# Retention queries of a hybrid decoder trunk: projected two token tiles at a time with channels on the partitions, and one sine table kept in SBUF

## The chip, the core and the metric

The kernel runs on one core of a Trainium2 chip. TensorE (PE) multiplies, VectorE (DVE), ScalarE (ACT) and GpSimd (POOL) work elementwise, SyncE (SP) issues most of the DMAs; each engine runs its own queue of instructions in order and waits on semaphores for the others. SBUF has 128 partitions; matmul results land in PSUM. The metric is the device time of one execution in microseconds (us); of several runs the median is given. The large products use the 32-bit type f32r, and to keep float32 accuracy each operand is split into a high and a low part and multiplied in three passes.

## What is computed

A trunk of two layers on 1024 tokens of 1024 channels. Each layer normalises x, projects it once into all the heads' inputs, runs three groups of heads (sliding-window attention, retention, gated linear attention) and projects their outputs back. The change touches retention: four heads of 64 channels, rotated by position, with a decay of its own per head.

```python
def apply_rotary(x, positions, inv_freq):
    ang = positions[..., None] * inv_freq
    cos, sin = jnp.cos(ang), jnp.sin(ang)
    x1, x2 = jnp.split(x, 2, axis=-1)
    return jnp.concatenate([x1 * cos - x2 * sin, x2 * cos + x1 * sin], axis=-1)

def step(state, inp):
    qi, ki, vi = inp
    sc = jnp.einsum('bhid,bhjd->bhij', qi, ki) * dmask
    intra = jnp.einsum('bhij,bhjv->bhiv', sc, vi)
    inter = jnp.einsum('bhid,bhdv->bhiv', qi * q_decay, state)
    new_state = chunk_decay * state + jnp.einsum('bhjd,bhjv->bhdv', ki * k_decay, vi)
    return new_state, intra + inter
...
rq = apply_rotary(rq.reshape(B, S, RET_HEADS, RET_DK), positions, ret_freq)
rk = apply_rotary(rk.reshape(B, S, RET_HEADS, RET_DK), positions, ret_freq)
r = retention(rq, rk, rv.reshape(B, S, RET_HEADS, RET_DV))
r_out = rms_norm(r).reshape(B, S, RET_W) * jax.nn.silu(rg)
```

`step` runs over chunks of 128 tokens. The attention's queries and keys are rotated in the same way with other frequencies.

## The kernel before

The tokens are 8 tiles of 128, in 4 pairs. For each pair the normalised tokens lie transposed in SBUF (channels on partitions, `hT`), as a high and a low part. A projection of one tile to 256 columns (`project`) keeps the token tile stationary and moves the weights: 3 passes over 8 blocks of channels, 24 matmuls of 256 columns, with tokens on the partitions of the result. `project_T` does the opposite for attention and gated linear attention: weights stationary, tokens moving, channels on the partitions of the result.

A layer runs through stages: the gates (`do_gates`: the columns rg and gg, silu by tanh), retention, gated linear attention, attention, output. In the retention stage (the loop at the end of the printed part of `layer`) each pair takes rq, rk and rv for its two tiles. `ret_rot` (L1154) rotates q and k with the tokens on partitions (`rotary`, five VectorE operations L823 to L828) and multiplies by the decay of the token within its chunk (L1157, tables qdec and kdec). `ret_core` (L1160) is a job for each tile: it transposes q and k on TensorE (two 128-wide transposes each, helper L180), copies all four out of PSUM in one 512-wide copy on ScalarE (helper L149, "rT"), makes the scores (helper L165, out of which VectorE takes the causal part, L1179), then the output po from the state stR and from the scores times v, and brings the state up to date (L1198, L1200). The output is normalised by head in `head_norm_gate`, with `rstd_of` (L632) for the reciprocal root.

The sines and cosines of all positions (`tables`, L411) are made once, while layer 0's gates run: one multiplication, 13 steps that reduce the angle, two sines on ScalarE (L438, L439, with a load of the function table), and two operations for the cosine. They lie in `sincos` with tokens on partitions; columns 0 to 31 of each tile are attention's, 32 to 63 retention's. For attention's queries, which lie with channels on partitions, `tables_T` (L444) copies each pair's sines four times over (L449), transposes them on TensorE (4 times 4), and stores them in DRAM (`tabS`); `attn_rot` loads them from there for every half (L864).

The order of TensorE's instructions is written by hand. The program counts a clock `clk` of TensorE's own work; jobs (Python generators) yield how long after the present clock they may go on, from the table `L`, and flags say what must have been reached. `pump()` lets those jobs run that are due, every `CHUNK` = 7 matmuls of a projection and after each projection. The order of the other engines' queues is set by the Tile framework's scheduler from priorities and its own estimates, so that an edit in one place moves instructions elsewhere. Buffers come from tagged pools: `t2` (512 wide), `t1` (256 wide), `aux` and `mm` (PSUM banks), `arena` (weights and tokens as high and low parts). Weights come by DMA into `st` and are split there: the high part by a copy on ScalarE (L149) or VectorE (L151), the low part by a subtraction (L533). The tokens of tiles 4 to 7 are normalised (`pre`) while the gates of the tiles before them run: squares L651, transposes L180, scale and shift L698 (ScalarE, first half) and L700 (VectorE, second half), high part L704, low part L708.

## Time and profile before

| | before |
|---|---|
| runs | 996.72, 998.21, 999.19 us; median 998.21 |
| profiled execution | 996.31 us, span of the trace 994.6 us, granted TensorE clock 0.991 |
| TensorE, VectorE, ScalarE, GpSimd busy | 965.7, 683.2, 409.3, 246.3 us |
| TensorE matmul records | 7133, of which 128-wide transposes (L180) 292 |
| gate stage of layer 0 | about 50 to 100 us |
| retention stage | about 103 to 195 us (layer 0), 595 to 676 us (layer 1) |

How to read the rows in the next parts: a window row gives the stretch, its length, then the busy time and instruction count of PE, PEld (weight loads, which overlap), DVE, ACT and POOL, then the granted clock, the share of the DMA engines, and GB/s. A timeline row gives the start, the duration, the engine, the source line, the operation, out<-in and how many instructions stand together; in brackets is how long the engine was idle just before and what it waited for. A row of the waits names the engine and line that waited, what for, the us in all, how often, and the longest. A row of the groups ends in the busy time, the mean duration in ns, and the idle time before.

### The profile page before, as it was taken

To read this page: it belongs to the slowest core of one execution; us is meant where nothing else is said; L and a number is where in the kernel's file an instruction comes from. 1 tells how busy PE (TensorE), PEld (TensorE's weight loads), DVE (VectorE), ACT (ScalarE), POOL (GpSimd) and SP (SyncE) were. 2 spreads that over 40 slices of the span, in tenths; PEclk is the share of its full clock that TensorE was granted. 3 is DMA by queue.
4 is the path that set the end of the run, shared out by engine and by line. 5 is a ranking of instruction groups with operands and counts; after the bars stand their busy time and mean duration, and the time that the engine had idled before them with its cause. 6 is when DMAs were issued, how large, how long until landed. Compare 5 with 4: busy or idle time off the path is not lost.

```text
span 994.6 us, 19641 instructions
## 1 busy us (share of the span) xinstructions
PE 965.7 (97%) x7133; PEld 824.3 (83%) x7133; DVE 683.2 (69%) x1679; ACT 409.3 (41%) x1152; POOL 246.3 (25%) x310
## 2 busy tenths in 40 slices
PE   5899999999999999999999999999999999999996
PEld 1599999888998777778889999988999877777785
DVE  3779857677766777664677286775766577567876
ACT  2477312233332656632555332133333257574222
POOL 2322001233310234420124101113322034545000
PEclk8899999999999999999999999999999999999999
DMA  9843513523135355587555241352122434378883
GB/s 321 290 138 97 159 44 115 177 86 121 61 100 166 91 157 168 170 274 239 189 170 171 69 150 38 118 157 83 53 93 86 127 91 133 112 235 266 267 262 139
DMA packets 112305, 148.77 MB, mean 150 GB/s; under 512 B 12065, under 2 KB 63821, under 8 KB 112209
## 3 DMA queue, kind: packets, MB, share of 16 engines
q1 hardware_dynamic: 106512, 137.96, 44.5%
q10 hardware_dynamic: 5696, 9.56, 2.6%
q8 instruction: 56, 0.92, 0.4%
q14 instruction: 41, 0.33, 0.1%
HBM read 109.20 MB, written 36.18 MB: 146 GB/s over the span
## 4 chain that ended last, share of the span: by engine, by line
PE 80%; DVE 7%; DMA 7%; issue 2%; POOL 1%; ACT 1%; SPq 0%; ACTq 0%; POOLq 0%; DVEq 0%
PE mm L165 61%; PE aux L165 14%; PE aux L180 5%; DMA st<-in_w_in_dram 2%; POOL sm L635 1%; DMA t<-aoS 1%; DMA st<-in_w_last_dram 1%; DMA xk<-in_x_dram 1%; DVE arena L533 1%; DMA a<-mixS 1%; DVE t L1248 0%; DVE t L328 0%; DMA t<-in_x_dram 0%; DMA t<-xs 0%; DMA mixS<-t 0%
## 5 line engine op out<-in xcount | busy, mean ns | idle before, releaser
L165 PE MATMUL mm<-arena 128*128 128x256 f32 (+2 forms) x1824 | 299.9, 318 | 1.8 <-ACT arena L704 1.8
L165 PE MATMUL mm<-arena,arena 128*128 128x256 f32 (+2 forms) x1824 | 298.2, 316 | 0.0
L165 PEld LDWEIGHTS mm<-arena 128*128 128x128 f32 x1824 | 255.5, 191 | 26.0 <-issue 3.3
L165 PEld LDWEIGHTS mm<-arena,arena 128*128 128x128 f32 x1824 | 252.2, 188 | 24.3 <-issue 3.7
L635 POOL TENSOR_TENSOR sm<-sm,mhalf 128x1 f32<-128x1 f32 (+1 forms) x64 | 55.8, 872 | 335.9 <-DVE sm L634 317.8
L165 PE MATMUL mm<-arena,mx 128*128 128x512 f32 (+1 forms) x564 | 130.6, 387 | 0.5 <-ACT kept L1341 0.5
L165 PEld LDWEIGHTS mm<-arena,mx 128*128 128x128 f32 x564 | 101.4, 188 | 24.7 <-issue 1.9
L149 ACT ACTIVATE t<-aux 128x256 f32<-128x256 f32 (+2 forms) x124 | 55.8, 468 | 73.8 <-PE aux L180 62.2
L149 ACT ACTIVATE arena<-st 128x512 fp32r<-128x512 f32 x94 | 56.2, 627 | 53.2 <-DMA st<-in_w_in_dram 19.4
L929 POOL TENSOR_TENSOR smx<-smx,sm 128x512 f32<-128x512 f32 x32 | 36.1, 1129 | 125.7 <-DVE sm L928 118.0
L533 POOL TENSOR_TENSOR arena<-st,arena 128x512 fp32r<-128x512 f32 x31 | 42.7, 1378 | 79.7 <-ACT arena L149 72.9
L533 DVE TENSOR_TENSOR arena<-st,arena 128x512 fp32r<-128x512 f32 x77 | 58.0, 775 | 5.2 <-ACT arena L149 3.3
L925 ACT ACTIVATE smx<-smx,sm 128x129 f32<-128x129 f32 x128 | 49.9, 393 | 25.9 <-DVE sm L922 25.7
L364 DVE SCALAR_TENSOR_TENSOR acc<-st,c_act,acc 128x512 f32<-128x512 f32 x60 | 46.7, 778 | 16.9 <-DMA st<-in_w_mod_dram 16.5
L180 PE MATMUL aux<-c_ident,t 128*128 128x128 f32 (+1 forms) x292 | 48.2, 282 | 5.4 <-DVE t L666 5.0
L180 PEld LDWEIGHTS aux<-c_ident,t 128*128 128x128 f32 (+1 forms) x292 | 35.0, 144 | 12.4 <-DVE t L666 6.9
L698 ACT ACTIVATE t<-aux,mod,mod 128x128 f32<-128x128 f32 x68 | 25.9, 459 | 43.0 <-DVE t L1248 18.1
L165 PEld LDWEIGHTS aux<-t,mx 32*128 32x128 f32 (+1 forms) x896 | 39.5, 187 | 3.9 <-issue 2.1
L973 ACT ACTIVATE t<-aux 128x256 f32<-128x256 f32 x32 | 12.3, 383 | 73.6 <-PE aux L165 65.0
L165 PE MATMUL aux<-t,mx 32*128 32x32 f32 (+1 forms) x896 | 40.7, 272 | 0.0
L920 DVE COPY_PREDICATED smx<-c_curmask,aux 128x256 f32<-128x256 int32 x64 | 25.4, 446 | 19.5 <-ACT smx L149 17.2
L1248 DVE SCALAR_TENSOR_TENSOR t<-t,sm,t 128x512 f32<-128x512 f32 x32 | 24.0, 780 | 18.2 <-DMA t<-in_x_dram 10.8
(224 smaller groups left out, 1387.7 us busy)
## 6 DMA issues: line engine op xcount, KB each, us to landing
st<-in_w_in_dram SPq DMA_DIRECT2D x96, 256.0 KB, 3.8
st<-in_w_mod_dram SPq DMA_DIRECT2D x64, 256.0 KB, 3.1
mx<-mixS SPq DMA_DIRECT2D x20, 512.0 KB, 4.9
mixS<-t SPq DMA_DIRECT2D x72, 128.0 KB, 3.7
st<-in_w_last_dram SPq DMA_DIRECT2D x36, 256.0 KB, 3.8
wm<-in_w_mod_dram SPq DMA_DIRECT2D x12, 512.0 KB, 7.0
t<-in_x_dram SPq DMA_DIRECT2D x24, 256.0 KB, 4.9
t<-tabS SPq DMA_DIRECT2D x16, 256.0 KB, 4.6
```

The costliest lines, as they stand in the source:

```text
L149: A.activation(dst, src, AF.Copy)
L165: T.matmul(dst, lhsT, rhs, start=start, stop=stop)
L180: T.transpose(dst, src, idn)
L364: V.scalar_tensor_tensor(acc, wt, c_act[:, k:k + 1], acc, ALU.mult, ALU.add)
L533: e.tensor_tensor(lo, st, f(hi), ALU.subtract)
L635: G.tensor_tensor(r, r, mhalf[:, :w], ALU.pow)
L698: A.activation(hf[:, ks], at[kt], AF.Identity, scale=gain, bias=shift)
L920: V.copy_predicated(sv, curmask.unsqueeze(1).to_broadcast((P, 2, P)), pv[:, :, n // P - 1, :])
L925: A.activation(sm[:, h, :], sm[:, h, :], AF.Exp, bias=mx[:, h:h + 1], accum_out=sums[:, h:h + 1])
L929: eng("pn").tensor_tensor(sm[:, :, 0:128], sm[:, :, 0:128], rs.unsqueeze(2).to_broadcast((P, 4, P)), ALU.mult)
L973: A.activation(sq, po, AF.Square)
L1248: V.scalar_tensor_tensor(xt[j], yg[j], r, xt[j], ALU.mult, ALU.add)
```

## The change

- Retention's queries are projected for a pair at once, with weights stationary and the pair's 256 tokens moving (`project_P`), so that the result has channels on partitions: two halves of 128 channels, 24 matmuls of 256 columns each. q is no longer transposed.
- The rotation of that result (`ret_q`) exchanges the two 32-channel halves of each head, that is, blocks of 32 partitions. Four VectorE products of 32 partitions by 512 read one block of PSUM and write the neighbouring block of SBUF; one 512-wide product with the cosines and one addition complete it. The result goes into a tile that borrows the buffer of attention's keys (tag kT0 or kT1).
- The decays leave q and k. A token's output only scales with q's decay and is normalised by head afterwards, so that the decay goes into the eps of that norm (`reps`); k's decay is put on v (`vdec`), where the ScalarE copy of v becomes a VectorE product.
- The copy of the transposed keys is 256 wide in place of 512 for q and k, and it and the causal product have high priority.
- `sincos` is transposed as it is (8 transposes in place of 16, no copies), stored to `tabS`, read back into `tab` (SBUF, 1 MB, four DMAs) for retention, and copied from DRAM to DRAM into `tabA` (two DMAs) for attention.
- The tables are made earlier (tb1 6.0 in place of 24.5) in one buffer of another pool.

```diff
     def tables():
-        ang = t2()
-        V.tensor_tensor(ang.rearrange("p (t k) -> p t k", t=NT), posf.unsqueeze(2).to_broadcast((P, NT, 64)),
-                        freq.unsqueeze(1).to_broadcast((P, NT, 64)), ALU.mult)
+        tmp = mix_tile(F32).rearrange("p a k q -> p (a k q)").rearrange("p (i n) -> p i n", i=4)
+        ang, nn, n2, red = (tmp[:, i] for i in range(4))
+        with tc.issue_after(mark[3].ins):
+            V.tensor_tensor(ang.rearrange("p (t k) -> p t k", t=NT), posf.unsqueeze(2).to_broadcast((P, NT, 64)),
+                            freq.unsqueeze(1).to_broadcast((P, NT, 64)), ALU.mult)
...
     def tables_T():
-        for p in range(NP_):
-            yield L["tt1"]
-            rep_ = t2()
-            V.tensor_copy(rep_.rearrange("p (s t h k) -> p s t h k", s=2, t=2, h=4),
...
+        for i in range(2):
+            yield L["tt1"] if i == 0 else L["tt2"]
             pt = aux()
-            for i in range(4):
-                transp(pt[:, i * P:(i + 1) * P], rep_[:, i * P:(i + 1) * P], ident)
+            for t in range(4):
+                transp(pt[:, t * P:(t + 1) * P], sincos[:, 4 * i + t].rearrange("p s k -> p (s k)"), ident)
             tb = t2()
             A.activation(tb, pt, AF.Copy, scale=0.125)
-            nc.sync.dma_start(tabS[p], tb.rearrange("p (s n) -> p s n", s=2))
+            ts = slice(512 * i, 512 * i + 512)
+            nc.sync.dma_start(tabS[:, :, :, ts].rearrange("s c k n -> (s c k) n"), tb)
+        yield L["tt3"]
+        for b in range(4):
+            nc.sync.dma_start(tab[32 * b:32 * b + 32], tabS[:, 1].rearrange("s k n -> k s n"))
+        yield 20.0
+        for j in range(2):
+            nc.sync.dma_start(tabA[:, :, j], tabS[j, 0].unsqueeze(0).to_broadcast((4, 32, S)))
...
+    def project_P(pm, l, p, w, c):
+        h = hT[(l, p)]
+        accum(pm, lambda a, k: w[:, a, k, c:c + P], lambda b, k: h[:, b, k, 0:256])
+
     def rstd_of(ss, w, scale, eps):
         r = small(w)
-        V.tensor_scalar(r, ss, scale, eps, ALU.mult, ALU.add)
+        if isinstance(eps, float):
+            V.tensor_scalar(r, ss, scale, eps, ALU.mult, ALU.add)
+        else:
+            V.scalar_tensor_tensor(r, ss, scale, eps, ALU.mult, ALU.add)
...
-            nc.sync.dma_start(d.rearrange("p (s n) -> p s n", s=2),
-                              tabS[2 * hf:2 * hf + 2, :, s, :].rearrange("s p n -> p s n"))
+            nc.sync.dma_start(d, tabA[:, :, s, 512 * hf:512 * hf + 512].rearrange("h k n -> (h k) n"))
...
-    def ret_rot(t, src, dec_):
+    def ret_q(l, p, w):
+        pm = mm()
+        for c in range(2):
+            project_P(pm[:, 256 * c:256 * c + 256], l, p, w, c * P)
+
+        def two(x):
+            return x.rearrange("p (c n) -> p c n", c=2)
+
+        sn, cs = (tab[:, i, 256 * p:256 * p + 256].unsqueeze(1).to_broadcast((P, 2, 256)) for i in range(2))
+        u, x = t2(), t2()
+        for b in range(4):
+            r = slice(32 * b, 32 * b + 32)
+            o = two(x)[32 * (b ^ 1):32 * (b ^ 1) + 32]
+            if b % 2:
+                V.scalar_tensor_tensor(o, two(pm)[r], -1.0, sn[r], ALU.mult, ALU.mult)
+            else:
+                V.tensor_tensor(o, two(pm)[r], sn[r], ALU.mult)
+        V.tensor_tensor(two(u), two(pm), cs, ALU.mult)
+        if p % 2 == 0:
+            rqT[0] = gp.tile([P, NT * P], F32, tag=f"kT{p // 2}", name=nm("rq"), bufs=1)
+        q = rqT[0][:, 512 * (p % 2):512 * (p % 2) + 512]
+        V.tensor_tensor(q, u, x, ALU.add)
+        flag(("rq", l, p), L["rq1"])
+        return two(q)
...
+    def ret_k(t, src):
         r = t1()
         rotary(r, src, 4, t, 1)
-        eng("rdec").tensor_tensor(h4(r), h4(r), dec_.unsqueeze(2).to_broadcast((P, 4, 64)), ALU.mult)
         return r

     def ret_core(l, t, q, k, v):
         yield lat("rc1", l)
         pt = aux()
         for j in range(2):
-            transp(pt[:, j * P:(j + 1) * P], q[:, j * P:(j + 1) * P], ident)
-            transp(pt[:, (2 + j) * P:(3 + j) * P], k[:, j * P:(j + 1) * P], ident)
-        tt_ = t2()
-        qT = tt_[:, 0:256]
-        kTt = tt_[:, 256:512]
-        copy("rT", tt_, pt)
+            transp(pt[:, j * P:(j + 1) * P], k[:, j * P:(j + 1) * P], ident)
+        kTt = t1()
+        with tc.high_priority():
+            copy("rT", kTt, pt[:, 0:256])
+        yield (0.0, ("rq", l, t // 2))
+        qT = q[:, :, P * (t % 2):P * (t % 2) + P]
...
                     if name == "rv":
                         v = t1()
-                        copy("rv", v, src)
+                        V.tensor_tensor(h4(v), h4(src), vdec.unsqueeze(2).to_broadcast((P, 4, 64)), ALU.mult)
...
-L = {... "tt1": 8.0, "tt2": 1.75, "tb1": 24.5, ...}
+L = {... "tt1": 7.0, "tt2": 2.0, "tt3": 2.0, "tb1": 6.0, "rq1": 6.5, ...}
```

The retention loop calls `ret_q` once per pair, ahead of the four projections of rk and rv. Lines behind the change have higher numbers (L698 becomes L708, L704 L714, L990 L999, L1198 L1234).

Three places where instructions move are shown. The first is ScalarE's queue in layer 0's gate stage, around the normalised tokens of tiles 4 and 5 (their high parts go into arena_320 before, arena_322 now). Before:

```order
L990 ACTIVATE t_138_770<-mm_700 128x256
L698 ACTIVATE t_143_797<-aux_792,mod_10_120,mod_11_121 128x128 x4
L651 ACTIVATE t_146_816,sm_818<-t_73_373 128x512
L704 ACTIVATE arena_320<-t_143_797 128x4x128
L651 ACTIVATE t_147_817,sm_818<-t_74_374 128x512
L704 ACTIVATE arena_320<-t_145_809 128x4x128
L990 ACTIVATE t_152_842<-mm_775 128x256
L1008 ACTIVATE gaT_417<-aux_867 48x128
```
And now, with the load of the sines' table, the two sines into `sincos`, and the load back for the tanh:

```order
L439 ACT_TABLE_LOAD
L439 ACTIVATE sincos<-mx_512 128x8x64
L440 ACTIVATE sincos<-mx_512 128x8x64
L708 ACTIVATE t_143_816<-aux_811,mod_10_122,mod_11_123 128x128 x2
L999 ACT_TABLE_LOAD
L999 ACTIVATE t_151_859<-mm_796 128x256
L714 ACTIVATE arena_322<-t_143_816 128x4x128
L661 ACTIVATE t_146_835,sm_837<-t_73_375 128x512
L661 ACTIVATE t_147_836,sm_837<-t_74_376 128x512
L1017 ACTIVATE gaT_419<-aux_881 48x128
L708 ACTIVATE t_156_896<-aux_891,mod_10_122,mod_11_123 128x128 x2
L714 ACTIVATE arena_322<-t_145_828 128x4x128
```
The table work now stands ahead of tile 5's two high parts; before, it stood some twenty rows behind them. On TensorE the gate projections of tiles 4 and 5 (mm_864 and mm_936) have the two groups of table transposes in between:

```order
L165 MATMUL mm_864<-arena_71,arena_322 128x272 x7
L180 MATMUL aux_891<-c_ident,t_132_748 128x128 x4
L180 MATMUL aux_903<-c_ident,t_133_749 128x128 x4
L165 MATMUL mm_864<-arena_71,arena_322 128x272 x3
L180 MATMUL aux_918<-c_ident,sincos 128x128 x4
L165 MATMUL mm_936<-arena_71,arena_322 128x272 x7
L180 MATMUL aux_944<-c_ident,ga_708 48x128
L165 MATMUL mm_936<-arena_71,arena_322 128x272 x14
L180 MATMUL aux_961<-c_ident,t_146_835 128x128 x4
L180 MATMUL aux_973<-c_ident,t_147_836 128x128 x4
L180 MATMUL aux_985<-c_ident,sincos 128x128 x4
L165 MATMUL mm_936<-arena_71,arena_322 128x272 x3
```
Before, tile 5's projection was broken there only by one transpose of the low-rank columns (ga), and the table's sixteen transposes came later.

The second place is VectorE in layer 0's retention, the query block of pair 3 (mm_2049 is the projection, rq_1851 the result) and the update of the state stR behind tile 4:

```order
L151 CAST arena_322<-st_2177 128x512
L536 TENSOR_TENSOR arena_322<-st_2177,arena_322 128x512
L1179 TENSOR_TENSOR t_354_2137<-mm_2049,tab 32x512
L1177 SCALAR_TENSOR_TENSOR t_354_2137<-mm_2049,tab 32x512
L1179 TENSOR_TENSOR t_354_2137<-mm_2049,tab 32x512
L1177 SCALAR_TENSOR_TENSOR t_354_2137<-mm_2049,tab 32x512
L1180 TENSOR_TENSOR t_353_2136<-mm_2049,tab 128x512
L1234 TENSOR_TENSOR stR<-stR,aux_2159 64x2x64
L1184 TENSOR_TENSOR rq_1851<-t_353_2136,t_354_2137 128x512
L1234 TENSOR_TENSOR stR<-stR,aux_2159 64x2x64
L984 TENSOR_REDUCE sm_2169<-t_359_2167 128x4
L1236 TENSOR_TENSOR stR<-stR,c_cdt 128x256
```
The update of stR (L1234, L1236) has the weights' cast and subtraction and five operations of the query block ahead of it in the queue.

The third is ScalarE at the end of layer 1's retention: the weights' high parts (arena_71, arena_320) and the copies of the transposed q and k of tiles 6 and 7 (t_1462, t_1475). Before:

```order
L149 ACTIVATE arena_71<-st_8316 128x2x256
L149 ACTIVATE t_1455_8232<-aux_8229 128x256
L149 ACTIVATE t_1456_8235<-aux_8229 128x256
L149 ACTIVATE t_1459_8248<-mm_8203 128x256
L149 ACTIVATE t_1462_8263<-aux_8258 128x512
L149 ACTIVATE t_1469_8302<-mm_8250 128x256
L149 ACTIVATE arena_320<-st_8363 128x512
L149 ACTIVATE t_1475_8323<-aux_8318 128x512
L149 ACTIVATE arena_320<-st_8380 128x512
L149 ACTIVATE arena_320<-st_8392 128x512
```
Now, with the key copies t_1431 and t_1444:

```order
L149 ACTIVATE arena_71<-st_8134 128x2x256
L149 ACTIVATE t_1424_8101<-aux_8098 128x256
L149 ACTIVATE t_1425_8104<-aux_8098 128x256
L149 ACTIVATE t_1431_8130<-aux_8127 128x256
L149 ACTIVATE arena_71<-st_8152 128x2x256
L149 ACTIVATE arena_71<-st_8183 128x2x256
L149 ACTIVATE t_1444_8188<-aux_8185 128x256
L982 ACTIVATE t_1448_8209<-aux_8194 128x256
L149 ACTIVATE arena_322<-st_8241 128x512
```
The key copy of tile 6 now stands ahead of two of the conversions into arena_71, and that of tile 7 ahead of the first into the other arena, behind which t_1475 stood before.

More of the change, by code (lines that the diff above doesn't have):

```diff
@@ L262, in trunk @@
     srS = dr.tile([NT, P, 256], F32, name="srS")
-    tabS = dr.tile([NP_, P, 2, 256], F32, name="tabS")
+    tabS = dr.tile([2, 2, 32, S], F32, name="tabS")
+    tabA = dr.tile([4, 32, 2, S], F32, name="tabA")
+    tab = cp.tile([P, 2, S], F32, name="tab")
     modc = {}
@@ L1203, in ret_core @@
         dma("lsr", sg, srS[t])
-        yield from head_norm_gate(l, t, po[:, 0:256], sg, 4.0 / 64.0, 4.0 * EPS, 4)
+        yield from head_norm_gate(l, t, po[:, 0:256], sg, 4.0 / 64.0, reps, 4)
     def y_half(l, t, nh, mixt, ss, yg):
@@ L1503, in layer @@
             last = p == NP_ - 1
-            rr = {}
-            for name in ("rq", "rk", "rv"):
+            q = ret_q(l, p, used(l, "rq"))
+            pump()
+            if last:
+                load(l, "gqk")
+            ks = {}
+            for name in ("rk", "rv"):
                 w = used(l, name)
```

36 lines of the change are left out of this document (16 added, 20 removed).

## The prediction

> **What bounds the kernel now.** I read the page first (span, busy shares, the chain's shares), then TensorE's waits, then the windows of the stages that the change touches, then the timelines at the places where a wait stands or may come.
>
> ```profile
> span 994.6 us, 19641 instructions
> PE 965.7 (97%) x7133; PEld 824.3 (83%) x7133; DVE 683.2 (69%) x1679; ACT 409.3 (41%) x1152; POOL 246.3 (25%) x310
> PE 80%; DVE 7%; DMA 7%; issue 2%; POOL 1%; ACT 1%; SPq 0%; ACTq 0%; POOLq 0%; DVEq 0%
> ```
>
> TensorE is busy for 97% of the span and 80% of the chain that ended last. So a matmul taken off shortens the time by itself, and work on any other engine costs something only where TensorE must wait for it. The windows say where that is near.
>
> ```profile
> core 0: us, PE busy (x) PEld busy (x) DVE busy (x) ACT busy (x) POOL busy (x), PEclk, DMA share, GB/s
> 65.00:70.00 5.00, 5.00 (x45) 5.00 (x44) 3.99 (x12) 5.00 (x15) 1.48 (x2) 1.00 0.74 225
> 70.00:75.00 5.00, 5.00 (x43) 4.98 (x42) 4.67 (x15) 4.76 (x15) 0.63 (x2) 1.00 0.13 43
> 100.00:170.00 70.00, 70.00 (x599) 67.84 (x598) 49.92 (x155) 16.45 (x34) 7.00 (x6) 1.00 0.34 105
> 170.00:200.00 30.00, 28.71 (x218) 26.50 (x217) 21.54 (x60) 9.57 (x20) 7.93 (x6) 1.00 0.53 161
> 595.00:660.00 65.00, 65.00 (x556) 63.18 (x556) 46.24 (x145) 14.97 (x31) 8.32 (x8) 1.00 0.26 81
> 660.00:680.00 20.00, 17.58 (x113) 14.79 (x113) 10.91 (x25) 6.10 (x15) 4.59 (x4) 1.00 0.56 167
> ```
>
> Retention runs from about 103 to 195 us and from 595 to 676 us. In its body TensorE never stops (70.00 of 70.00, 65.00 of 65.00), VectorE has 29% to spare and ScalarE 77%. Idle stands only at its two ends: 1.3 us after 170, 2.4 us after 660. The gate stage at 65 to 75 us is another case: TensorE is full there too, but ScalarE has 0.24 us of 10 free and VectorE 1.3 us. Whatever is added there runs into the end of the stretch.
>
> **The matmuls.** The unit prices are two pieces of the chain.
>
> ```profile
> 103.60 4.83 PE mm L165 x41
> 108.42 0.44 PE aux L180 x4
> ```
>
> A 256-wide product takes 4.83/41 = 0.118 us, a 128-wide transpose 0.11. The query projection has 24 products of 256 columns per tile before; now it has 24 for each of two channel halves over the pair's 256 tokens: 48 for a pair either way, cost nothing. The transposes of q go: 2 per tile, 8 tiles, 2 layers = 32. The tables take 8 transposes in place of 16. 40 x 0.11 = **-4.4 us**, and with TensorE full I see no cover that could swallow it other than a new wait.
>
> **The waits at the end of retention.**
>
> ```profile
> PE aux L165 <- ACT t L149: 3.0, 3, 1.3
> 192.83 0.71 PE L165 MATMUL aux<-t 64*128 64x128 f32 x8 [1.29 <-ACT t L149]
> 663.09 0.71 PE L165 MATMUL aux<-t 64*128 64x128 f32 x8 [0.54 <-ACT t L149]
> 669.66 0.71 PE L165 MATMUL aux<-t 64*128 64x128 f32 x8 [1.22 <-ACT t L149]
> 191.39 0.63 ACT L149 ACTIVATE arena<-st 128x512 fp32r<-128x512 f32 x1 [1.14 <-DMA st<-in_w_in_dram]
> 668.49 0.63 ACT L149 ACTIVATE arena<-st 128x512 fp32r<-128x512 f32 x1 [3.71 <-DMA st<-in_w_in_dram]
> 669.03 0.58 ACT L149 ACTIVATE t<-aux 128x512 f32<-128x512 f32 x1
> ```
>
> All three are scores that wait for the copy of the transposed q and k. At 669.03 it is seen why: the copy stands on ScalarE behind a weight conversion that waited 3.71 us for its DMA; at 191.39 the same with 1.14 us. Those copies were ready long before. In the changed order the key copy (256 wide) of the last tiles stands ahead of those conversions, in both layers. So the sum of the three, 1.29 + 0.54 + 1.22, goes: **-3.0 us**, with 0 as the other bound if the copy's own inputs (the transposes, which TensorE's hand-made order now places elsewhere) come no earlier, or if the scores then wait for the query block. I take all of it since the cause seen at 668.49 is an order and the order is changed.
>
> **VectorE in retention.**
>
> ```profile
> L823 DVE TENSOR_TENSOR t<-mm,sincos 128x256 f32<-128x256 f32 (+1 forms) x48 | 17.7, 369 | 6.0 <-ACT va L851 4.0 <-PE mm L165 1.9
> L825 DVE TENSOR_TENSOR tr<-mm,sincos 128x128 f32<-128x128 f32 (+1 forms) x48 | 12.3, 256 | 0.0
> L827 DVE TENSOR_TENSOR t<-t,tr 128x128 f32<-128x128 f32 (+1 forms) x48 | 12.6, 263 | 0.0
> L1157 DVE TENSOR_TENSOR t<-t,c_qdec 128x256 f32<-128x256 f32 x16 | 6.7, 418 | 0.2
> L870 DVE TENSOR_TENSOR t<-mm,t 128x512 f32<-128x512 f32 x16 | 11.0, 688 | 15.5 <-PE mm L165 11.8 <-DMA t<-tabS 3.6
> L873 DVE TENSOR_TENSOR t<-t,t 128x512 f32<-128x512 f32 x8 | 8.5, 1057 | 0.0
> L1198 DVE TENSOR_TENSOR stR<-stR,aux 64x128 f32<-64x128 f32 x28 | 7.9, 281 | 0.2
> 67.98 1.29 DVE L708 TENSOR_TENSOR arena<-t,arena 128x512 fp32r<-128x512 f32 x2 [1.01 <-ACT arena L704]
> 73.08 0.69 DVE L708 TENSOR_TENSOR arena<-t,arena 128x512 fp32r<-128x512 f32 x1
> ```
>
> One tile's rotation of q or k is 0.369 + 2 x 0.256 + 2 x 0.263 = 1.41 us (L826 and L828 repeat L825 and L827), with the decay 1.83. A pair has four: 7.3. Now a pair has two rotations of k without decay (2.8), two multiplications of v from PSUM, 256 wide (2 x 0.42 by L1157), and six 512-wide operations for q: 6 x 0.69 by L870 = 4.1. Together 7.8, so **+0.5 us per pair**; a pair lasts 17.5 us, of which 5 are free on VectorE, and ScalarE loses work. Hidden, cost nothing in the sum.
>
> What no row shows is a product of 32 partitions that is written to another block of partitions. Below: L1198 on 64 partitions takes 0.281 for 128 elements against L825's 0.256 on 128 partitions, so fewer partitions buy nothing, 0.69 stands as the floor. Above: L873, the slowest 512-wide row on this engine, 1.06. I take 0.69, since L870 has the same operands (PSUM and SBUF).
>
> The block does stand in a queue. In pairs 2 and 3 of layer 0 its first five operations come ahead of the update of the state stR, on which the next tile's output product waits. Back to back a 512-wide operation takes 1.29 - 0.69 = 0.60. VectorE needs 5 x 0.60 + 2 x 0.28 + 0.60 + 0.42 = 4.6 us from the end of the projection to the new state; TensorE's order gives it about 4.1 (24 products of the next projection, an output, a state product, a 512-wide row sum): short by 0.5. In pair 3 TensorE gives some 0.8 more, but a cast and a subtraction for the weights (about 1.0) stand in front of it: short by 0.7 to 1.1. The bounds are 0 (what stands ahead is done before the projection ends) and 1.7; I take **+0.8**. In layer 1 the updates stand ahead of the block: nothing.
>
> [...]
>
> **The sine table, moved.** This is the term that I trust least.
>
> ```profile
> 55.96 1.86 SPq L154 DMA_DIRECT2D srS<-t  x2
> 63.41 0.63 ACT L149 ACTIVATE arena<-st 128x512 fp32r<-128x512 f32 x1 [3.10 <-DMA st<-in_w_in_dram]
> 71.37 0.64 ACT L704 ACTIVATE arena<-t 128x512 fp32r<-128x512 f32 x1
> 72.87 0.64 ACT L704 ACTIVATE arena<-t 128x512 fp32r<-128x512 f32 x1 [0.24 <-DVE t L700]
> 73.68 1.49 PE L165 MATMUL mm<-arena,arena 128*128 128x272 f32 x10
> 76.31 0.68 DVE L423 SCALAR_TENSOR_TENSOR t<-t,t 128x512 f32<-128x512 f32 x1
> 72.75 0.42 DVE L418 TENSOR_SCALAR t<-t 128x512 f32<-128x512 f32 x1
> 86.47 1.28 ACT L1023 ACT_TABLE_LOAD   x1
> 87.76 0.63 ACT L1023 ACTIVATE t<-t 128x512 f32<-128x512 f32 x1
> 89.71 0.63 ACT L438 ACTIVATE sincos<-t 128x512 f32<-128x512 f32 x1
> 90.24 0.62 ACT L439 ACTIVATE sincos<-t 128x512 f32<-128x512 f32 x1
> ```
>
> Before, the 14 operations that reduce the angles lie between 69 and 88 us, and the two sines at 89.71, with slack behind them. Now they stand at some 53 to 72 us in VectorE's order, 9 of L423's kind and 5 of L418's: about 9 x 0.60 + 5 x 0.34 = 7.1 us pushed into the queue that also makes the low halves of the normalised tiles. On ScalarE a table load, the two sines and a load back (1.28 + 1.15 + 1.28 = 3.7 us) now stand between the second half of tile 4 and the first half of tile 5. In the window 65 to 75 that engine had 0.24 us free. TensorE needs tile 5's high half three products into the row at 73.68, at 74.0; before it was there at 71.37 + 0.64 = 72.0. The second half, there at 72.87 + 0.64 = 73.5, is used four products later, at 74.5. So the margins are 2.0 and 1.0 us, and 3.7 us of ScalarE plus the delay of VectorE are laid on them.
>
> A walk through both queues with these durations: the second query chunk may land earlier than 63.41, since its issue now stands ahead of the two stores that took 1.86 us; I take half of that, 62.5. ScalarE then reaches tile 4's second half at about 70.5 (it waits for VectorE's scaling, now behind the table), ends the sines at 72.9 and tile 5's halves at 75.8 and 78.8. TensorE comes to tile 5 at 74.9 (after 0.6 of wait for tile 4's low half and 0.4 for the four 128-wide transposes of the table), waits 0.9 for the first half, 2.5 for the second, and 0.6 for a PSUM bank at the second set of transposes. With the transposes counted above, the waits are 0.6 + 0.9 + 2.5 + 0.6 = **+4.6 us**. Bounds: 0, if ScalarE's queue is in fact ahead when the chunk does not hold it; 8.5, if the chunk lands at 63.4 (+0.9) and VectorE's operations with two SBUF inputs stretch as L873 does against L870 (9 x 0.37 = +3.3).
>
> [...]
>
> The rest costs nothing: the eps tables are constants in the same number of operations, the one SBUF table takes 1 MB of DMA and the attention's tables another 1 MB where the share is 0.13 to 0.34, and attention loads as many bytes as it did.
>
> **Sum.** -4.4 - 3.0 + 0.8 + 4.6 = -2.0 us. The profiled execution took 996.31 (span 994.6), so 994.3; the median of the runs, 998.21, lies 1.9 above it: **996.2 us**.
>
> **Rivals.** *The early waits do not come.* The walk rests on one chunk's landing and on the order in which two full queues get through; if the chunk lands 2 us earlier, or part of the table work falls into VectorE's gaps ahead of 63, that term shrinks to nothing: -6.6, **991.6**. For it: TensorE was 100% busy in every one of these windows. Against it: ScalarE's 0.24 free us.
>
> *The waits at the end of retention stay*, because the scores wait for what else is late there (the decayed v, the query block, the mask product): the -3.0 falls away, +1.0, **999.2**.
>
> *The early stage costs its upper bound.* Landing at 63.4 and stretched table operations, waits of 8.5: -4.4 - 3.0 + 0.8 + 8.5 = +1.9, **1000.1**; it ends slower than before once the waits there pass 6.6.
>
> *The crossing products cost the price of L873.* Slower than before, at one place: 4 x (1.06 - 0.60) = 1.8 us more in each block, which in pairs 2 and 3 of layer 0 stands directly ahead of stR: waits of 0.6 + 1.8 and 1.1 + 1.8 in place of the 0.8 taken, +4.5, so +2.5 in all, **1000.7**. It decides from 0.74 us per product back to back, if the two waits come whole (1.7 + 2 x 4 x 0.14 = 2.8, which with -4.4, -3.0 and 4.6 is nothing). For it: nothing here crosses partitions, and L873 shows 512-wide operations that are slow; against it: L873's operands are both in SBUF, these are not.
>
> **How the numbers follow.** Forecast 0.36 (its own range 994 to 998.5); early waits absent 0.29; end waits stay 0.12; early stage at its bound 0.12; crossing products 0.11. From 990.5 (the second case with the last waits of 0.3 to 0.4 us gone too) to 1002 (the slower cases with a microsecond more each) some 0.2 is left outside. 0.3%, 3.0 us, is what a measurement of this kernel tells from no change: faster is below 995.2, slower above 1001.2. Faster: the second case and 0.16 of the forecast, 0.45. Slower: half of the two cases at 1000 and 0.06 from the others' tails, 0.16. Same: 0.39.
>
> **What would show it.** 1: L180 on TensorE falls from 292 to 252. 2: no wait for L149's copy near 190, 663 and 669. 3: waits of 0.5 to 2.5 us for ScalarE's high halves between 70 and 80 us, a table load and two sines just before, about 4.6 in all; if that window is full, the second case. 4: the products of 32 partitions at 0.6 to 0.7 us; at 1.0 or more, the slower case. 5: a wait for stR in layer 0 under 1.2. Wrong altogether if TensorE idles at a new place in the body of retention, where I have put nothing.

## The result, and the profile after

The changed kernel takes 1011.73 us (median of 6 runs, 1009.15 to 1015.91) against 997.81 (996.56 to 999.19): a ratio of 1.0141, with a 95% interval of 1.0121 to 1.0160. It is slower by 14 us; forecast were 996.2 us and a range of 990.5 to 1002. The profiled execution took 1009.24 us, 12.9 more than the one before.

The page of the changed kernel, the lines on the span and the engines:

```profile
span 1007.5 us, 19483 instructions
PE 967.5 (96%) x7093; PEld 823.9 (82%) x7093; DVE 694.0 (69%) x1627; ACT 399.3 (40%) x1135; POOL 249.2 (25%) x310
```

The 40 matmul records less (7133 to 7093) are the transposes that were to go. Yet TensorE is busy 1.8 us longer, and idle for 40.0 us of the span in place of 28.9. What it waited for stands in the view of TensorE's waits (us in all, times, longest):

```profile
PE aux L180 <- DVE t L676: 6.6, 4, 4.0
PE mm L165 <- ACT arena L149: 6.3, 1, 6.3
PE mm L165 <- ACT arena L714: 4.6, 3, 1.8
PE aux L165 <- DVE stR L1236: 1.2, 2, 0.8
PE aux L165 <- ACT t L149: 1.1, 1, 1.1
PE mm L165 <- DVE t L1001: 1.0, 2, 0.7
PE mm L165 <- DVE t L1180: 0.9, 2, 0.6
PE aux L180 <- DVE mx L1130: 0.7, 1, 0.7
PE aux L165 <- DVE sm L281: 0.6, 1, 0.6
PE aux L180 <- DVE sincos L443: 0.4, 1, 0.4
PE mm L165 <- DVE arena L718: 0.3, 1, 0.3
```

The second row is new and the longest of all outside the start: one wait of 6.3 us for a weight that ScalarE splits. 1.8 us of the third row stood at 40 us before as well. The windows answer to those of the prediction:

```profile
65.00:70.00 5.00, 4.35 (x37) 4.13 (x37) 5.00 (x10) 4.59 (x15) 2.67 (x4) 1.00 0.46 140
70.00:75.00 5.00, 3.77 (x28) 3.32 (x28) 4.64 (x13) 3.98 (x7) 0.59 (x2) 1.00 0.23 77
100.00:170.00 70.00, 63.39 (x514) 61.13 (x513) 45.06 (x108) 11.31 (x25) 5.37 (x5) 0.93 0.31 100
170.00:200.00 30.00, 29.52 (x253) 28.74 (x251) 23.48 (x61) 6.25 (x14) 5.90 (x5) 1.00 0.37 115
595.00:660.00 65.00, 64.35 (x549) 62.10 (x548) 46.37 (x116) 11.03 (x26) 4.68 (x5) 1.00 0.28 84
660.00:680.00 20.00, 19.99 (x165) 19.25 (x165) 17.28 (x43) 5.04 (x11) 3.42 (x3) 1.00 0.39 120
```

The gate stage at 65 to 75 us has lost 1.9 us, as forecast. But the body of layer 0's retention, 100 to 170 us, which was full, has lost 6.6 us, and its mean granted clock is 0.93. This is the sign that the prediction named for being wrong altogether: TensorE idles at a new place in the body of retention.

TensorE's timeline shows where:

```profile
72.48 1.26 PE L165 MATMUL mm<-arena,arena 128*128 128x272 f32 x8 [0.94 <-ACT arena L714]
...
77.86 0.77 PE L165 MATMUL mm<-arena,arena 128*128 128x272 f32 x4
80.45 0.64 PE L165 MATMUL mm<-arena,arena 128*128 128x272 f32 x3 [1.83 <-ACT arena L714]
...
114.37 0.94 PE L165 MATMUL mm<-arena,arena 128*128 128x256 f32 x6 [0.28 <-DVE t L1180]
121.57 5.66 PE L165 MATMUL mm<-arena,arena 128*128 128x256 f32 x25 [6.26 <-ACT arena L149]
```

The first row is a wait for tile 4's second high half, ready at 71.80 + 0.63 = 72.43 in ScalarE's rows below; the walk had none there. The third is the wait for tile 5's second high half (79.77 + 0.63 = 80.40), 1.83 for the forecast 2.5. For tile 5's first half, ready at 77.80, TensorE did not wait: it came to it only at 77.86, behind the first set of table transposes. The last row is in the second rk projection of the first pair. ScalarE and SyncE's queue show the weight chunk for which it waited:

```profile
71.80 0.63 ACT L714 ACTIVATE arena<-t 128x512 fp32r<-128x512 f32 x1
72.45 1.28 ACT L439 ACT_TABLE_LOAD   x1
73.74 0.63 ACT L439 ACTIVATE sincos<-mx 128x512 f32<-128x512 f32 x1
75.61 1.28 ACT L999 ACT_TABLE_LOAD   x1
77.18 0.62 ACT L714 ACTIVATE arena<-t 128x512 fp32r<-128x512 f32 x1
79.77 0.63 ACT L714 ACTIVATE arena<-t 128x512 fp32r<-128x512 f32 x1
...
120.88 0.63 ACT L149 ACTIVATE arena<-st 128x512 fp32r<-128x512 f32 x1 [9.75 <-DMA st<-in_w_in_dram]
```

```profile
105.82 1.39 SPq L461 DMA_DIRECT2D tabA<-tabS  x2
107.25 0.63 SPq L154 DMA_DIRECT2D st<-in_w_in_dram  x1
```

The last quarter of the weights of rk was issued at 107.25 and used by ScalarE at 120.88: 13.6 us, where such loads before took 3.8 in the median from issue to landing:

```profile
st<-in_w_in_dram SPq DMA_DIRECT2D x96, 256.0 KB, 3.8
```

It stands directly behind the two copies into `tabA`. The view of the DMA engines over 112 to 119 us, in 40 slices (tenths of the 16 engines' time, and GB/s):

```profile
DMA  9756996774433222222223222222222576889743
GB/s 375 281 152 176 269 281 257 269 246 176 176 129 129 117 94 117 117 94 94 94 94 140 94 117 117 94 94 94 117 117 94 152 176 199 246 316 339 304 176 152
```

For half of that time two to three tenths of the engines are busy, at about 100 GB/s, while the weight chunk is awaited. The view gives only the mean of the engines; a share of a quarter would be 4 of 16, and `tabA`'s copies have 4 repeats as their outermost dimension. At 100 GB/s the 1 MB takes 10 us: about the delay of the chunk. That these copies lie on 4 engines is my estimate from the share and the 4 repeats; no view lists the engines one by one. Where loads of weights stand nearly alone, 123.5 to 126.5 us, the same view has slices of nine tenths and more.

The wait has a second price, in windows of 2 us (the clock stands before the last two numbers):

```profile
114.00:116.00 2.00, 1.03 (x7) 0.77 (x6) 2.00 (x8) 0.00 (x0) 0.00 (x0) 1.00 0.27 109
116.00:118.00 2.00, 0.00 (x0) 0.00 (x0) 1.68 (x6) 0.00 (x0) 0.00 (x0) 0.70 0.38 123
118.00:120.00 2.00, 0.00 (x0) 0.00 (x0) 0.00 (x0) 0.00 (x0) 0.00 (x0) 0.50 0.47 182
122.00:124.00 2.00, 2.00 (x11) 2.00 (x11) 1.95 (x2) 0.00 (x0) 1.44 (x1) 0.50 0.12 45
```

The granted clock falls to 0.50 in the wait and is still there when TensorE works again: 11 products in 2 us, and the 25 products at 121.57 take 5.66 us in place of 25 x 0.118 = 2.95. That is 2.7 us more. The last product before the wait ended at 114.37 + 0.94 = 115.31, and the clock fell about 1.5 us later (1.00 over 115 to 116 us, 0.90 on average over 116 to 117, 0.50 from 117 on).

So the accounts of the two profiled executions, in us: transposes -4.4 (40 x 0.11), gate stage +4.5 (0.4 + 0.3 + 1.0 and 4.6 - 1.8), the rk chunk +6.3 and its clock +2.7, end waits -1.9 (3.05 to 1.13), the state +0.9 (1.2 for 0.3), the PSUM bank that the query block holds +0.9 (L1180), and 2.0 of small waits in the stages behind (L1130, L281 and 1.3 of the first row, where 0.6 stood before). That makes +11.0; the other 1.9 of the 12.9 I could not place.

### The profile page after: what moved, and what is told of

Its sections match the earlier page's. It is cut to its first block, busy times and chain, and to the rows that moved or that the text cites. A ratio compares the mean times of both kernels' runs of the same rounds, so it can differ in the third digit from the quotient of the medians.

```text
span 1007.5 us, 19483 instructions
## 1 busy us (share of the span) xinstructions
PE 967.5 (96%) x7093; PEld 823.9 (82%) x7093; DVE 694.0 (69%) x1627; ACT 399.3 (40%) x1135; POOL 249.2 (25%) x310
## 4 chain that ended last, share of the span: by engine, by line
PE 58%; DMA 7%; DVE 7%; ACT 2%; issue 1%; POOL 1%; SPq 0%; ACTq 0%; POOLq 0%; DVEq 0%
PE mm L165 43%; PE aux L165 12%; PE aux L180 3%; DMA t<-in_x_dram 2%; DMA st<-in_w_last_dram 1%; DVE t L1284 1%; DVE arena L536 1%; DMA st<-in_w_in_dram 1%; DMA a<-mixS 1%; DMA st<-in_w_mod_dram 1%; DMA t<-aoS 1%; ACT t L708 1%; DMA t<-mixF 1%; POOL sm L645 0%; DVE arena L718 0%
## 5 line engine op out<-in xcount | busy, mean ns | idle before, releaser
L165 PE MATMUL mm<-arena,arena 128*128 128x256 f32 (+2 forms) x1824 | 301.9, 318 | 10.3 <-ACT arena L149 6.3
L165 PEld LDWEIGHTS mm<-arena,mx 128*128 128x128 f32 x564 | 101.4, 188 | 24.5 <-issue 1.2
L149 ACT ACTIVATE t<-aux 128x256 f32<-128x256 f32 (+2 forms) x124 | 51.9, 440 | 103.4 <-PE aux L180 85.5
L149 ACT ACTIVATE arena<-st 128x512 fp32r<-128x512 f32 x94 | 56.2, 628 | 67.5 <-DMA st<-in_w_in_dram 35.1
L536 DVE TENSOR_TENSOR arena<-st,arena 128x512 fp32r<-128x512 f32 x77 | 61.6, 818 | 6.0 <-ACT arena L149 3.2
L180 PE MATMUL aux<-c_ident,t 128*128 128x128 f32 (+1 forms) x244 | 42.3, 286 | 7.6 <-DVE t L676 6.6
L708 ACT ACTIVATE t<-aux,mod,mod 128x128 f32<-128x128 f32 x68 | 26.3, 460 | 46.5 <-DVE t L1284 20.2
L180 PEld LDWEIGHTS aux<-c_ident,t 128*128 128x128 f32 (+1 forms) x244 | 29.9, 146 | 14.8 <-DVE t L676 7.2
```

The source lines that it names most:

```text
L149: A.activation(dst, src, AF.Copy)
L165: T.matmul(dst, lhsT, rhs, start=start, stop=stop)
L180: T.transpose(dst, src, idn)
L536: e.tensor_tensor(lo, st, f(hi), ALU.subtract)
L708: A.activation(hf[:, ks], at[kt], AF.Identity, scale=gain, bias=shift)
```

## The experiments

All times are medians, beside runs of the kernel before on the same chip; ratios are to it. Profiles are one execution each. One line of the whole diff is in no experiment by itself: the changed kernel also sets `dynamic_dma_scratch_size=1024`. All kernels below carry it, and the pages before and after list the same four DMA queues.

**The copies spread over the engines** (e1_spread); the queues of all engines keep their order.

```diff
-            nc.sync.dma_start(tabA[:, :, j], tabS[j, 0].unsqueeze(0).to_broadcast((4, 32, S)))
+            nc.sync.dma_start(tabA[:, :, j].rearrange("h k n -> k h n"), tabS[j, 0].unsqueeze(1).to_broadcast((32, 4, S)))
```

> The changed kernel, the two DRAM to DRAM copies into tabA written with the 32 channels as the outer dimension in place of the 4 repeats; the order on every engine is the same. Theory A: the copies ran on about 4 of the 16 DMA engines for some 10 us (100 GB/s at a share of 0.25), and the weight chunk for rk, which needs all 16, stood behind them on those 4; spread out they take about 2.5 us, the 6.3 us wait and the 2.7 us of slow clock after it go: 1002 to 1003.5. Rival B: it is the 1 MB through memory, whatever the engines: the wait stays above 4 us, 1008 or more. Rival C: the chunk is issued too late (107.3 us) and is slow by itself: no change, 1011.

1012.36 us (1004.46 to 1017.94, 4 runs), 1.0131 (1.0065 to 1.0197). In its waits the row in question is now:

```profile
PE mm L165 <- ACT arena L149: 1.5, 1, 1.5
```

The shape of the copies made 4.8 of the 6.3 us, since nothing else differs; that is theory A. The remaining 1.5 speaks for a part of B: in this trace the chunk, issued at 106.5, is used at 115.8, still 9 us, with the DMA engines over nine tenths busy for several of them. The time did not follow. The four executions lie at 1004.5, 1007.3, 1017.4 and 1017.9, the last two with a mean clock of 0.976 and 0.977 against 0.986 and 0.989. The profiled one was of these, and its windows and timeline show what happened to it, in the gated linear stage:

```profile
229.00:284.00 55.00, 53.65 (x500) 49.86 (x500) 32.41 (x109) 14.57 (x48) 13.04 (x23) 0.75 0.27 85
250.00:260.00 10.00, 10.00 (x89) 9.60 (x89) 5.28 (x13) 2.40 (x9) 3.61 (x6) 0.51 0.41 135
```

```profile
251.59 2.79 PE L165 MATMUL aux<-t,mx 32*128 32x32 f32 x48
254.73 5.37 PE L165 MATMUL mm<-arena,arena 128*128 128x256 f32 x24
```

The 48 small products took 1.54 us at full clock in the kernel before, 24 products of 256 columns 3.06. No wait above 0.75 us stands in this stage. So there is a loss besides the waits: at 0.75 of the clock over these 55 us TensorE loses a quarter of them, some 13.7 us, and this execution's span (1015.7) is 13.0 above that of the fastest of the four (1002.7). It comes in some executions and not in others.

**The copies 30 us later**, in their first shape (e2_late).

```diff
-        yield 20.0
+        yield 50.0
         for j in range(2):
```

> The changed kernel, the two copies in their first form but 30 us later by the hand-made clock, behind all four rk chunks on SyncE's queue. Theory A: the rk wait goes as in the run before, 1002 to 1004.5; the copies still take 10 us on 4 engines, but only chunks of the next layer's modulation stand behind them. Rival B: the same gain. Rival C: the rk wait stays, 1011.

1007.09 us (1003.23 to 1014.49, 4 runs), 1.0112 (1.0065 to 1.0159). The wait for the rk chunk is gone, only 0.3 us is left there, so rival C falls: the chunk is not slow by itself. The profiled execution has a span of 1001.3 us, 6.2 under the changed kernel's, and took 1003.2, within theory A's numbers; the median is above them, in part by the low clock again (1014.5 with 0.976; another took 1005.8 with 0.991). Theory A and rival B forecast the same here, so this run does not tell them apart.

**The table 8 and 14 us later**, with the spread copies (e3_tb14, e3_tb20).

```diff
-"tb1": 6.0
+"tb1": 14.0
```

> The spread copies, and the sine table begun 8 us later (tb1 14 in place of 6). If the 4.4 us of waits in the gate stage come from the table work standing in ScalarE's and VectorE's queues ahead of tiles 4 and 5, they shrink by half or more: 2 to 4 us under the spread kernel. If they come from the late landing of the query weights or from the two further VectorE waits alone, no change from the spread kernel.

> The spread copies, and the table begun 14 us later (tb1 20). The gate stage's waits go (4 us under the spread kernel) if the table's place makes them; against it, the table comes back into SBUF only about when the first query block needs it: a new wait there of 0 to 4 us if the two stores, four loads and their landing (some 8 us) end behind the first projection.

With 14.0: 1001.55 us (999.41 to 1011.97, 10 runs), 1.0073 (1.0040 to 1.0106). Of the 4.5 us of waits in the gate stage 1.7 are left (0.25 for ScalarE's high half, 1.43 for a small copy on ScalarE at 84 us), so the table's place made them. The median is 10.8 us under that of e1, more than these waits: two of e1's four executions were at the low clock. With 20.0: 1002.52 us (999.41 to 1004.10, 5 runs), 1.0054 (1.0035 to 1.0073). The gate stage waits 0.15 us, and the forecast other wait is there: 1.18 us for VectorE at 111 us, 0.39 for the first query block at 118, and 1.10 for the state at 131. The table costs TensorE at either end.

**The new table alone** (t_table), **the new retention alone** (r_ret), **and both moves of the copies with the table 8 us later** (c1_both). The first two are the kernel before with one half of the change each; the third has the edits of e1, e2 and e3_tb14 together.

```diff
+    tab = cp.tile([P, 2, S], F32, name="tab")
...
+    G.memset(tab, 0.125)
```

(The lines by which r_ret fills its table.)

> The kernel before with the new sine table alone (made early, 8 transposes, tab and tabA written as in the change); retention as before, with q rotated on token partitions and transposed, so tab is loaded and never read. Theory A, the loss is the table's: waits of about 4.4 us in the gate stage and a late weight chunk in the first pairs of retention (6 to 9 us with the slow clock after it), less 0.9 for the transposes: 1006 to 1011. Rival D, the loss is retention's own: 997 to 1001.

> The kernel before with the new retention alone; the tables as before, at their old place, and the table that the query block reads in SBUF is filled with a constant once at the start (it leaves out making that table from the positions, so the rotation of q has constant factors). Theory A: 32 transposes less (-3.5) and 1 to 3 us of the waits at the end of retention, less 1 us of new waits for the state and for the PSUM bank: 991 to 995. Rival D: the query block itself brings new waits (bank held for 3.5 us, state behind the block, later VectorE in the stages that follow) that eat all of it: 996 to 1002.

> The changed kernel with the copies into tabA spread over 32 rows, 30 us later, and the table begun 8 us later. With neither the rk wait nor most of the gate waits: 997 to 1001 in undisturbed executions, as the kernel with the table alone moved by 8 us (998.2 us of span), or 1 us less if the copies still delayed a chunk there.

The table alone: 1008.66 us (1007.85 to 1011.23), 1.0121 (1.0078 to 1.0164), as theory A had it. Its waits hold both losses, with the old retention behind them:

```profile
PE mm L165 <- ACT arena L149: 6.8, 1, 6.8
...
PE mm L165 <- ACT arena L707: 4.6, 3, 1.8
```

The retention alone: 1005.19 us (1002.08 to 1009.48), 1.0069 (1.0043 to 1.0095), on rival D's side and beyond it. Two of its waits, 4.15 and 1.59 us, are for VectorE's copies for the old attention table (L450), which come late once the query block is in the queue, and the clock is at 0.66 on average over 110 to 120 us, around the first. So it was not yet a clean case. All three together, c1: 1000.08 us (997.85 to 1009.10, 10 runs), 1.0037 (1.0009 to 1.0064), within its forecast of 997 to 1001 and the best of the whole changed kernels, and still not faster than before.

**The retention alone, with that wait out of the way** (r2_ret: tt2 7.0; r3_ret: tt1 32, tt2 5), and c1 with other places of the table and the state's update given priority (c2_16, c2_12).

```diff
-            for c in range(2):
+            with tc.high_priority():
+                for c in range(2):
...
-"tb1": 14.0
+"tb1": 16.0
```

> The kernel with the new retention alone and the constant table (it leaves out making that table), with the attention table's transposes put 5 us further behind their copies (tt2 7.0), since two waits of 4.2 and 1.6 us for those copies, with the slow clock after the first, stood in the first such kernel. Theory A: without these waits the new retention is worth its 32 transposes and some of the end waits: 992 to 996. Rival D: the later waits that this retention brings (the gated linear stage, the normalisation ahead of layer 1) eat it: 996 to 1000.

> The kernel with spread and later copies (c1), the table begun 2 us later still (tb1 16) and the update of the state given high priority, so that it stands ahead of the query block. The 0.5 us state wait and part of the 1.4 us gate wait go: 996 to 999 undisturbed, against 998 to 1000 for c1. If the later table is too late for the first query block, a new wait near 110 us and 999 to 1002.

> The same with the table begun at 12: if the gate wait comes from the table work's place, it grows again by 1 to 2 us against tb1 16: 998 to 1001.

r2: 1007.56 us (1004.09 to 1011.41), 1.0106 (1.0073 to 1.0139). Neither theory's number: with the copies put off, TensorE waited 4.14 us at 113 us for L1180, the last product that frees the query projection's PSUM bank. c2_16: 1002.51 us (998.61 to 1009.41, 9 runs; a tenth took 1016.50 at a mean clock of 0.974), 1.0056 (1.0031 to 1.0081); c2_12: 1003.84 us (999.84 to 1010.30, 7 runs), 1.0070 (1.0043 to 1.0097). The state's wait in layer 0 went in both, but 1.5 us for the key copy (L149) came at 190 us in its place, and the gate stage waited 3.4 and 3.1 us against c1's 1.7, at other instructions. Two misses: work moved that nobody had in mind, and the gate's waits did not follow the table's place. Both kernels differ from c1 in the priority and in that place, so which of the two moved it is not shown.

> The new retention alone with the constant table (it leaves out making that table), and the four copies and sixteen transposes for attention's table spread out to 24 us and more behind the start of retention (tt1 32, tt2 5). In the two kernels before this one VectorE was still making the old table when the first query block came, and TensorE waited 4.1 us for the block to free a PSUM bank or for the copies. With the copies out of the way that wait falls to 2 us or less and no cold clock follows: 994 to 999. If it stays at 4 us and the median above 1002, the wait is the query block's own and not the table's.

r3: 1005.12 us (1002.91 to 1008.57, 7 runs), 1.0078 (1.0053 to 1.0104). The wait for the bank fell to 1.7 us as expected, the time did not. Its waits:

```profile
PE aux L165 <- ACT t L149: 3.0, 2, 1.7
PE mm L165 <- DVE t L1180: 2.3, 2, 1.7
PE aux L165 <- DVE mx L1130: 2.2, 1, 2.2
PE aux L165 <- DVE sm L642: 2.0, 1, 2.0
```

These four make 9.5 us, where the kernel before had 3.0 (L149), 0.2 (its mx) and 0.4 (its sm): 5.9 more. 32 transposes, 3.5 us, pay for somewhat over half of that. Behind the third the clock falls as well, to 0.82 on average over 220 to 230 us and 0.84 over 230 to 240, which costs another 3.4 (1.8 + 1.6). Together that is 5.8 of the 8.0 us by which this profiled span (1002.6) exceeds the one before.

**The new table alone, with the copies spread and later** (t2_table).

> The new table alone, as before, with the copies into tabA spread over 32 rows and 30 us later. Theory A: of the 10 us that the new table costs, the 6.85 us wait for the rk chunk and the slow clock after it go and the 4 us of gate waits stay: 1000 to 1002. Rival C (the chunk is late by SyncE's order): the wait stays, 1006 or more.

1001.21 us (997.01 to 1003.46, 10 runs), 1.0033 (1.0012 to 1.0053): theory A. Of the table's 10 us, 7.5 are the two copies (1008.66 to 1001.21; 6.4 if each median is taken against its own runs of the kernel before, 998.55 and 997.51). The rest is the gate stage, whose waits stand as they were (4.6 us for L707 again).

**Half of the query block taken away** (k1_r3_one from r3, k2_c1_one from c1).

```diff
-        for b in range(4):
...
+        V.tensor_tensor(two(x), two(pm), sn, ALU.mult)
```

> The new retention alone with the constant table (r3), with one product of 128 partitions by 512 in place of the four crossing products of 32 (it leaves out the exchange of the halves, so q is not rotated rightly); matmuls, transposes and waits on data stay. The block on VectorE falls from six to three operations, 4.1 to 2.0 us a pair. Theory E, the block's length on VectorE makes the new waits (1.7 us for the PSUM bank, 2.0 for the state, 2.2 in the gated linear stage): they fall by half or more, 997 to 1001. Rival F, the waits come from the order that the scheduler finds for the new program, not from the length: no change from r3, 1003 to 1006.

> The same one product in the kernel with early table and the copies spread and later (c1; the exchange of the halves left out). Theory E: c1's remaining waits in the first pair, for the state and behind the block in layer 1 (0.5 to 0.6 each) go and the kernel falls by 2 to 5 us, to 995 to 998, below the kernel before. Rival F: within 1 us of c1's 1000.

k1: 1004.39 us (1003.16 to 1006.57), 1.0074 (1.0050 to 1.0099). k2: 1003.09 us (1002.67 to 1004.05), 1.0055 (1.0037 to 1.0074). VectorE worked 19 us less in k1 than in r3 (675.0 for 694.0 us), and the time fell by 0.7. In k1 the bank's wait is gone and others stand in its place:

```profile
PE aux L165 <- ACT t L149: 2.6, 2, 2.3
PE mm L165 <- ACT kept L1371: 2.2, 1, 2.2
PE aux L165 <- DVE mx L1130: 2.2, 1, 2.2
PE aux L165 <- DVE t L1209: 1.5, 1, 1.5
```

Theory E falls: with half of the block's operations gone neither kernel reached its numbers, so the block's length is not what eats the transposes' gain. Rival F had k1 right and missed k2, which came out 3 us above c1 and not within 1 (1.0055 for 1.0037, intervals that overlap), with a wait of 2.97 us for L149 at 196 us where c1 has none. Both runs fit F's argument, that each new program comes out with an order of its own around the hand-made one, and with waits of 1 to 3 us at other places; which rule of the scheduler makes them was not tried, and F is not shown further than that.

## Why the prediction was wrong

- **Transposes, -4.4**: right in number (7133 to 7093 records; in layer 1, two transposes less per tile bring the next product some 0.2 us sooner).
- **The sine table, +4.6**, the term that I trusted least: right in sum, +4.5, and in its cause, since the later table of e3_tb14 took 2.8 us of these waits away. The table load, the two sines and the load back stand ahead of tile 5's high halves (72.45 to 76.89 in ScalarE's timeline); the halves are ready at 77.8 and 80.4, 2 us behind the walk's 75.8 and 78.8. But that the sum came out is in part luck. Of the walk's four waits, 0.6 for tile 4's low half was 0.29 (L718), 0.9 for tile 5's first half did not come, 2.5 for its second was 1.83, and 0.6 for a PSUM bank at the second set of transposes was 0.40 for the table itself (L443) at the first set: 2.5 in place of 4.6. The other 1.9 stand where the walk had nothing: 0.94 for tile 4's second high half and 1.0 for L1001 on VectorE, whose queue holds the table's operations too.
- **The end of retention, -3.0**: -1.9. The waits of 1.29 in layer 0 and 0.54 in layer 1 went, the last became 1.13. I read the key copy of tile 7 as standing ahead of the conversion into arena_322, which it does, and overlooked that one into arena_71 stands right ahead of it; that one now waits 3.66 us for its DMA (at 682.42 us), and the copy behind it.
- **The state, +0.8**: +0.9 (0.48 in layer 0, 0.75 in layer 1, where I had put none, less the 0.30 before); in layer 0 alone, for which the 0.8 was worked out, it is 0.48, so the sum agrees in part by luck.
- **VectorE's products, 0.69 each**: right. The timeline of the first block:

```profile
112.12 0.69 DVE L1179 TENSOR_TENSOR t<-mm,tab 32x512 f32<-32x512 f32 x1
112.82 0.69 DVE L1177 SCALAR_TENSOR_TENSOR t<-mm,tab 32x512 f32<-32x512 f32 x1
113.53 0.69 DVE L1180 TENSOR_TENSOR t<-mm,tab 128x512 f32<-128x512 f32 x1
114.14 0.41 DVE L833 TENSOR_TENSOR t<-mm,sincos 128x256 f32<-128x256 f32 x1
```

One starts 0.70 after the other, while L833 starts 0.61 after L1180: the overlap, 0.09 between 512-wide operations before (1.29 - 0.69 = 0.60 from start to start) and 0.08 in the last pair here, is missing from one crossing product to the next, and from the last of them to L1180 (0.71). By these rows that costs 0.4 us a block; what makes it was not tried.

- **The step that failed** is the sentence "The rest costs nothing": one MB for attention's tables "where the share is 0.13 to 0.34". I took the mean share of the engines for room. By my estimate from their share of 0.25 and their outermost 4 these copies are not spread over the engines but fill about 4 of 16, and a chunk that was issued behind them 1.4 us later came some 10 us late; with the copies spread TensorE's wait was 1.5 us, with the copies 30 us later it was gone. That is +6.3 us of wait and +2.7 of clock, and, by the table alone with and without that, 7.5 of the 14 us. I had counted the DMAs' bytes, not their shape, their place on SyncE's queue and who stands behind them, though the diff shows the 4 as the first dimension of `tabA`. No rival had it.
- **What no term had**: TensorE behind the query block (0.9 for the bank that the block holds for five operations), and 2.0 us in the gated linear stage and in the normalisation ahead of layer 1, where the change has no line. With the copies and more than half of the gate waits out of the way (c1) the ratio is 1.0037, not the forecast's 0.998.
- **The slower rivals** were priced too low: both ended near 1000, since each took one mechanism and left the clock at 1.00. The range was built on waits alone.

What stays open: 1.9 us of the profiled difference; why the new retention with the table left out costs 7 to 11 us (r_ret, r2, r3) in place of the 5 to 6 that the forecast's own terms for it would save, of which r3's profile shows the waits and the low clock but not why they come where they come; and what brings the low clock in the gated linear stage in some executions.

## What to carry to other kernels

Of a DMA, read the outermost dimension and what is issued behind it, before its bytes: here 1 MB at a quarter of the engines' time held up the chunk behind it by some 10 us, at a mean share that looked like room, and with 32 in place of 4 outermost the wait of 6.3 us was 1.5. A stall on a full TensorE costs more than its length once the clock falls: here the wait of 6.3 us cost 9.0. Where one engine's order is written by hand and the others' found by a scheduler, a term of the sum that rests on a wait going away should carry the chance that it comes back elsewhere.

## What the runs showed of the hardware

- In the changed kernel's idle stretch of 6.3 us the granted clock fell to 0.50 about 1.5 us after the last product (0.90 over 116 to 117 us, 0.50 over 117 to 118), was still 0.50 over 126 to 127 us and 0.98 over 127 to 128: full again some 5.5 us after work began. A short wait does not decide alone: behind the 1.82 or 1.83 us for the high half near 80 us the mean clock over 80 to 90 us was 0.83 in e2_late and t_table, where the 14 products next in the row took 2.97 and 3.23 us, and 1.00 in the changed kernel, e1 and t2, where they took 2.00.
- In the gated linear stage, where TensorE has runs of 32x32 products, the clock was 0.51 over 250 to 260 us in one execution (e1) with no idle time in that window, and 1.00 in the changed kernel's. By the mean of 0.81 over 240 to 250 us it had fallen at about 246, 1 us behind a wait of 0.61. Waits alone do not explain it: in k2 the mean clock was 0.87 over 220 to 230 us with TensorE busy for 9.91 of the 10.00, and in the changed kernel, e2_late and e3_tb14 waits of 0.5 to 1.1 us in this stage brought no fall (1.00 in every 10 us from 200 to 290). Of the kernel before, the 69 executions beside these experiments stayed between 993.8 and 1002.0 us; of c1, 8 of 10 lay under 1002.4 and two at 1007.1 and 1009.1, with mean clocks of 0.981 and 0.982.
- A product that writes another block of 32 partitions takes what the same width takes in place: 0.69 us for 512 columns, with 32 partitions as with 128 (L1179 and L1177 against L1180 in the changed kernel at 112 to 114 us).
